# Where the second and third layer's input products are made in a four-layer trunk

## The chip, the cores and the metric

The kernel runs on one core of one Trainium2 chip. The time is device microseconds of one execution of the whole program; the median of the runs is given. The profile is one further execution, recorded by the hardware profiler. Five engines work beside each other and meet at semaphores: TensorE (PE) with its weight loads (PEld), VectorE (DVE), ScalarE (ACT), GpSimd (POOL) and SyncE (SP). SP issues most DMA transfers; POOL and ACT issue some.

## The reference

A trunk of four layers over 256 positions of width 1024, all in float32. Each layer adds three things to the residual h: a mixer (S5 state space in layers 0 and 3, attention with forget gates in layer 1, gated linear attention in layer 2), an MLP with squared ReLU, and a gated input embedding:

```python
for i in range(DEPTH):
    h = h + mixer_i(rmsnorm(h, norm_mix[i]))
    h = h + jnp.square(jax.nn.relu(rmsnorm(h, norm_mlp[i]) @ mlp_w1[i])) @ mlp_w2[i]
    gate = jax.nn.sigmoid(rmsnorm(h, norm_ple[i]) @ ple_gate[i])
    h = h + (p[i] @ ple_proj[i]) * gate
return rmsnorm(h, final_norm)
```

`p[i]` is an input of 256 positions by 256, `ple_proj[i]` a weight of 256 by 1024. Their product depends on nothing that the trunk computes, so it can be made at any time before the gate needs it.

## The kernel before

h stays in SBUF, transposed, as four tiles `HH` of 128 x 2 x 256. A big product streams its weight in units of 256 x 512 (512 KB). `unit` (L149) loads a unit into a tile `raw` (three buffers), ACT casts it to a rounded `whi` (L157), and DVE subtracts to get the rest, `wlo` (L159); each of the two has four buffers. The other operand is split the same way into two halves by `scaled` (L367, L368). `col` (L173 to L175) then makes three float32r matmuls in place of one exact product: hi x hi, hi x lo, lo x hi. `dense` runs such units over two column blocks and hands the finished PSUM tiles to an eviction function. The MLP uses a variant, `wide` (L209, L211).

An exact float32 matmul without the split is used in two places of the first S5 layer, "plain": the S5 input weights (`plain_block`, L261) and the input product of layer 0 (`plain_ple_proj`, L439 to L457). It needs no cast and no subtraction, and takes `raw` directly.

The embedding stage is `ple` (L459): it takes the input product `pp`, scales h, and makes the gate product with `ple_gate[l]`; the function `gate` (L472 to L479) multiplies by the normalisation, applies the sigmoid on ACT (L477), multiplies by `pp` (L478) and adds to h (L479). Where `pp` comes from differs by layer. For layers 0 and 3 it is made inside the S5 mixer (step p0 or p3) and waits in `pp_done`. For layers 1 and 2 `ple` calls `ple_proj` (L428) at its start: load `p`, split it on ACT and DVE, load and split two weight units, 48 matmuls, four copies out of PSUM (L436). So these products stand on PE between the last product of the MLP and the first product of the gate.

The first S5 layer is written out by hand as a list of steps, `FIRST` (L26). Four channel blocks b = 0 to 3 are passed through the steps w (input product, then the tile U by DMA), f (fetch of that block's S5 parameters, issued by POOL), i (input matrices and rotation, DVE), o (output matrices, DVE, with in-block products on PE, L922 to L927), s (states: 64 products, L972, then some ten DVE operations L708 to L989), y (outputs: products L1007, a GELU on ACT, transposes L1019, a split into `g`). Step p0 is the plain input product. After the list come the GLU products on `g` in `dense`, with the outputs of block 3 in their midst.

The order that the program gives is a priority: a scheduler with a simulated clock fixes each engine's order beforehand, taking among what it thinks ready the work that was written first. On the chip each engine follows that order strictly and waits where something isn't there. PSUM tiles are shared out by tags: `acc` and `wk` have three buffers, `po` and `mk` one each. The input products, the states of odd blocks and the transposes of `g` all take `acc`. `self.load` issues a transfer on SP behind the last weight unit.

Of the kernel before, what the change touches and what calls it, by code (L numbers as in the profile page):

```python
# [9 lines left out]
F32 = mybir.dt.float32  # L10
# [7 lines left out]
T, D, FF, DEPTH = 256, 1024, 4096, 4  # L18
# [4 lines left out]
        "acc": 3, "wk": 3, "po": 1, "mk": 1}  # L23


FIRST = "f0 w0 o0 w1 i0 w2 w3 f1 s0 i1 o1 s1 p0 f2 i2 y0 o2 s2 y1 f3 i3 o3 s3 y2"  # L26
LATER = "w0 i0 o0 w1 i1 o1 w2 s0 i2 w3 s1 p3 y0 o2 s2 i3 y1 o3 s3 y2"

HELD = 2
# [29 lines left out]
class Trunk:  # L59


    def __init__(self, ctx, tc, A):
        self.tc, self.nc, self.A = tc, tc.nc, A
        nc = self.nc
        pool = lambda name, **k: ctx.enter_context(tc.tile_pool(name=name, **k))
        self.const = pool("const", bufs=1)
        self.wp = pool("wp", bufs=4)
        self.sc = pool("sc", bufs=2)
        self.dram = pool("dram", bufs=1, space=bass.MemoryType.DRAM)
        self.sm = pool("sm", bufs=4)  # L70
        self.pp = pool("pp", bufs=4, space=PSUM)
        self.kept = self.ahead = self.last_unit = None
        self.lo_after = []
        self.pp_done = {}
        P = 128
        const = lambda name, shape, dt=F32: self.const.tile(shape, dt, name=name)
        self.lam = self.s5_load(0)
        self.gains = const("gains", [P, 3 * DEPTH + 1, 8])
        nc.sync.dma_start(self.gains, A["gains"])
        self.HH = [const(f"h{k}", [P, 2, T]) for k in range(4)]  # L80
        self.H = [self.HH[k // 2][:, k % 2] for k in range(8)]
        for k in range(4):
            nc.sync.dma_start(self.HH[k], A["xT"][k * 256:(k + 1) * 256, :].rearrange("(k p) t -> p k t", p=P))
        self.ident = const("ident", [P, P])
        make_identity(nc, self.ident)
        self.mhalf = const("mhalf", [P, 1])
        nc.gpsimd.memset(self.mhalf, -0.5)
        self.mean = const("mean", [P, 1])
        nc.gpsimd.memset(self.mean, 1.0 / D)
        self.ones = const("ones", [P, P])  # L90
        nc.gpsimd.memset(self.ones, 1.0)

        self.blk = const("blk", [P, 2])
        nc.gpsimd.affine_select(self.blk[:, 0:1], self.ones[:, :1], [[0, 1]], ALU.is_ge, 0.0, base=63, channel_multiplier=-1)
        nc.gpsimd.affine_select(self.blk[:, 1:2], self.ones[:, :1], [[0, 1]], ALU.is_ge, 0.0, base=-64, channel_multiplier=1)
        self.nblk = const("nblk", [P, 2])
        nc.gpsimd.tensor_scalar(self.nblk, self.blk, -1.0, None, ALU.mult)
        self.eye16 = const("eye16", [32, 16])
        nc.vector.tensor_tensor(self.eye16, self.ident[0:32, 0:16], self.ident[0:32, 16:32], ALU.add)
        self.zero = const("zero", [1, 512], BF16)  # L100
        nc.gpsimd.memset(self.zero, 0.0)
        self.halfpi = const("halfpi", [P, 1])
        nc.gpsimd.memset(self.halfpi, math.pi / 2)
        self.tms = [const(f"tm{i}", [P, 8, 4, 16]) for i in range(3)]
        for t in self.tms:
            nc.gpsimd.memset(t, 0.0)
# [329 lines left out]
        self.dense(x, A["ple_proj"][l], lambda n, ps: nc.scalar.copy(out[n // 2][:, n % 2], ps))  # L436
        return [out[n // 2][:, n % 2] for n in range(4)]

    def plain_ple_proj(self, l):  # L439

        nc, A = self.nc, self.A
        x = self.a2("praw", (128, 2, T))
        self.load(x, A["pT"][l].rearrange("(k p) t -> p k t", p=128))
        out = []
        for cb in range(2):
            raw = self.wp.tile([128, UK, 512], F32, name="raw", tag="raw", bufs=BUFS["raw"])
            self.last_unit = nc.sync.dma_start(raw, A["ple_proj"][l][:, cb * 512:(cb + 1) * 512].rearrange("(k p) n -> p k n", p=128))
            t = self.t4("pp", (128, 2, 2, T))
            for i in range(2):
                ps = self.psum((128, 2, T), "acc")  # L450
                for n in range(2):
                    for k in range(2):
                        c = (2 * i + n) * 128
                        nc.tensor.matmul(ps[:, n], raw[:, k, c:c + 128], x[:, k], start=k == 0, stop=k == 1)
                nc.scalar.copy(t[:, i], ps)
            out += [t[:, 0], t[:, 1]]
        return out  # L457

    def ple(self, l):  # L459
        nc, A = self.nc, self.A  # L460
        pp = self.pp_done.pop(l, None) or self.ple_proj(l)
        x = self.scaled(2 * DEPTH + l)
        sq = self.squares()
        v = {}

        def rows():
            v["rows"] = self.rstd_rows(sq)

        def rstd():
            v["r"] = self.rstd(v["rows"])  # L470

        def gate(n, ps):  # L472
            z = self.t2("z", (128, 2, T))

            for i in (slice(0, 1), slice(1, 2)) if l == DEPTH - 1 and n > 1 else (slice(0, 2),):
                nc.vector.tensor_tensor(z[:, i], ps[:, i], v["r"].unsqueeze(1).broadcast_to([128, i.stop - i.start, T]), ALU.mult)
                nc.scalar.activation(z[:, i], z[:, i], AF.Sigmoid)  # L477
                nc.vector.tensor_tensor(z[:, i], z[:, i], pp[n][:, i], ALU.mult)  # L478
                nc.vector.tensor_tensor(self.HH[n][:, i], self.HH[n][:, i], z[:, i], ALU.add)  # L479

        self.dense(x, A["ple_gate"][l], gate, mid={1: rows, 2: rstd}, tags=("acc", "wk"))
# [568 lines left out]
    def s5(self, l):  # L1050
        nc, A = self.nc, self.A
        j = l // 3
        first = self.kept is None
        us = []

        def w_in(b):
            w = A["s5_w_in"][j]
            ps = self.plain_block(x, w, b, q["mark"]) if first else self.block(x, w, b)
            u = self.t2("u", (128, 2, 4, 64))
            nc.vector.tensor_tensor(u.rearrange("x k s j -> x k j s"), ps.rearrange("x k (j s) -> x k j s", s=4),  # L1060
                                    r.rearrange("x (j s) -> x j s", s=4).unsqueeze(1).broadcast_to([128, 2, 64, 4]), ALU.mult)
            us.append(self.s5_inputs(u.rearrange("x k s j -> x k (s j)")))
# [14 lines left out]
        def make_in(b):  # L1077
            d0 = decay(b)
            if first:
                rot = drain(self.s5_rot(q, b))  # L1080
                return drain(self.s5_in(b, *parts[b][0:2])), rot, d0
            win = fetch(b, 0, (128, 2, 8, 64), "win")
            return [[win[:, i]] for i in range(2)], fetch(b, 1, (128, 2, 8, 64), "m4"), d0

        def make_out(b):
            if first:
                return self.s5_inside(b, *drain(self.s5_way_out(q, b, parts[b][2])))
            out = fetch(b, 2, (128, 2, 4, 8, 16), "m4")
            return [out[:, i] for i in range(2)], self.s5_lags(b, self.kept[0][b, 3, 0:32, 0:512].rearrange("x (p f) -> x p f", p=8), nc.sync)
# [16 lines left out]
        def step(what, b):  # L1106
            if what == "w":
                w_in(b)
            elif what == "f":
                parts[b] = self.s5_fetch(j, q, b)  # L1110
            elif what == "i":
                ins.append(make_in(b))
            elif what == "o":
                outs.append(make_out(b))
            elif what == "s":
                states.append(self.s5_states(b, us[b], *ins[b], first))
            elif what == "p":
                self.pp_done[l] = self.plain_ple_proj(l) if first else self.ple_proj(l)
            elif what == "y":
                gT.extend([] if gT else self.ktiles("g"))  # L1120
                self.s5_outputs(b, *states[b], *outs[b], gT)

        for t in (FIRST if first else LATER).split():
            step(t[0], int(t[1]))
# [122 lines left out]
```

## Time and profile before

| | |
|---|---|
| median of 3 runs | 1461.5 us (1461.08 to 1461.75) |
| the profiled execution, its own time | 1461.99 us |
| its span, first to last instruction | 1460.2 us |
| mean granted TensorE clock | 0.984 of full speed |
| DMA | 255.06 MB, 175 GB/s in the mean |

How to read the rows that follow. A line of the timeline has start and duration in us, the engine, the line of the program, the operation, the tile written and the tiles read, the shape, and a count; in brackets stands how long the engine was idle before it and what ended that. A row of the windows view has the window, its length, then for PE, PEld, DVE, ACT and POOL the busy us with the number of instructions in brackets, then the granted clock, the share of the 16 DMA engines and GB/s. A row of groups has the busy us, the mean ns of one, and the idle time before them with what ended it. PE's matmuls are pipelined: one can last 0.28 us by its record while the next starts 0.12 us after it, so start times tell the rate, durations don't.

### The profile page before, as it was taken

What the parts mean: (1) busy time and instruction counts of PE and PEld (TensorE: products, weight loads), DVE (VectorE), ACT (ScalarE), POOL (GpSimd) and SP (SyncE); (2) the same over time, 40 slices, a digit from 0 to 9 for tenths busy, and PEclk for the clock granted to TensorE, in tenths of its full rate; (3) what the DMA queues carried; (4) which work ended last, traced back from release to release, by engine and by line L of the source; (5) the groups of instructions that cost most, each with busy time, mean ns of one, the idle gap of its engine ahead of it and who ended that gap; (6) DMA issues with size and microseconds to landing.
All of it is one profiled execution on the core that took longest, in us unless ns stands there. A gap on an engine that the chain in (4) does not pass through costs nothing. (4 is left out here: it accounts for less than half of the span.)

```text
span 1460.2 us, 26622 instructions
## 1 busy us (share of the span) xinstructions
PE 1403.9 (96%) x10734; PEld 1266.9 (87%) x10734; DVE 1054.3 (72%) x1739; ACT 723.2 (50%) x1118; POOL 86.8 (6%) x142
## 2 busy tenths in 40 slices
PE   7889999999999999999999999999997899999998
PEld 6779988889999888888989588888997899888898
DVE  8994578767776578887676468886777946766665
ACT  3233565445655654545566455454563345545443
POOL 3100000010000000010004000100000000000020
PEclk9999999999999999999999999999999899999999
DMA  6623555566554347775555446774665446566551
GB/s 211 198 81 119 186 176 189 187 203 191 175 151 142 108 153 236 230 228 180 188 164 157 132 129 190 234 229 150 222 246 152 137 141 185 179 188 187 173 191 69
DMA packets 146347, 255.06 MB, mean 175 GB/s; under 512 B 24768, under 2 KB 35296, under 8 KB 146224
## 3 DMA queue, kind: packets, MB, share of 16 engines
q1 hardware_dynamic: 132912, 234.35, 50.8%
q0 software_dynamic: 5248, 17.31, 3.7%
q10 hardware_dynamic: 8064, 1.71, 0.6%
q8 instruction: 84, 1.38, 0.4%
q14 instruction: 39, 0.32, 0.1%
HBM read 242.68 MB, written 7.86 MB: 172 GB/s over the span
## 5 line engine op out<-in xcount | busy, mean ns | idle before, releaser
L159 DVE TENSOR_TENSOR wlo<-raw,whi 128x1024 fp32r<-128x1024 f32 x406 | 494.2, 1226 | 289.0 <-ACT whi L157 283.9
L157 ACT CAST whi<-raw 128x1024 fp32r<-128x1024 f32 x406 | 422.5, 1049 | 453.4 <-PE mk L209 77.7
L209 PE MATMUL wk<-x,whi 128*128 128x512 f32 x576 | 182.4, 401 | 7.5 <-DVE relu L220 7.5
L211 PEld LDWEIGHTS wk<-x,wlo 128*128 128x128 f32 x576 | 106.8, 190 | 23.1 <-issue 0.2
L209 PE MATMUL acc<-s,whi 128*128 128x512 f32 x384 | 118.5, 395 | 0.0
L211 PE MATMUL wk<-x,wlo 128*128 128x256 f32 x576 | 113.3, 281 | 0.0
L173 PE MATMUL acc<-x,whi 128*128 128x256 f32 x352 | 99.8, 288 | 4.6 <-DVE u L1060 2.9
L209 PEld LDWEIGHTS wk<-x,whi 128*128 128x128 f32 x576 | 92.2, 192 | 11.5 <-DVE relu L220 8.6
L174 PE MATMUL acc<-x,whi 128*128 128x256 f32 x352 | 100.3, 287 | 0.0
L175 PE MATMUL acc<-x,wlo 128*128 128x256 f32 x352 | 100.1, 286 | 0.0
L211 PEld LDWEIGHTS acc<-s,wlo 128*128 128x128 f32 x384 | 70.3, 188 | 15.8
L209 PE MATMUL mk<-x,whi 128*128 128x512 f32 x256 | 81.5, 395 | 0.0
L211 PE MATMUL acc<-s,wlo 128*128 128x256 f32 x384 | 74.3, 280 | 0.0
L173 PEld LDWEIGHTS acc<-x,whi 128*128 128x128 f32 x352 | 67.6, 194 | 6.4 <-issue 4.1
L175 PE MATMUL wk<-s,wlo 128*128 128x256 f32 x256 | 72.4, 283 | 0.0
L174 PE MATMUL wk<-s,whi 128*128 128x256 f32 x256 | 72.4, 283 | 0.0
L173 PE MATMUL wk<-s,whi 128*128 128x256 f32 x256 | 72.4, 283 | 0.0
L175 PEld LDWEIGHTS acc<-x,wlo 128*128 128x128 f32 x352 | 68.1, 194 | 0.1
L174 PEld LDWEIGHTS acc<-x,whi 128*128 128x128 f32 x352 | 68.0, 194 | 0.2
L209 PEld LDWEIGHTS acc<-s,whi 128*128 128x128 f32 x384 | 59.6, 189 | 1.4
L209 PE MATMUL po<-s,whi 128*128 128x512 f32 x192 | 60.7, 396 | 0.0
L209 PE MATMUL wk<-s,whi 128*128 128x512 f32 x192 | 60.1, 395 | 0.0
(399 smaller groups left out, 3376.0 us busy)
## 6 DMA issues: line engine op xcount, KB each, us to landing
raw<-mlp_w SPq DMA_DIRECT2D x256, 512.0 KB, 4.3
raw<-s_w_glu SPq DMA_DIRECT2D x32, 512.0 KB, 3.6
raw<-ple_gate SPq DMA_DIRECT2D x32, 512.0 KB, 3.6
raw<-fox_w_in SPq DMA_DIRECT2D x24, 512.0 KB, 3.8
raw<-gla_w_in SPq DMA_DIRECT2D x24, 512.0 KB, 3.6
raw<-s_w_out SPq DMA_DIRECT2D x16, 512.0 KB, 4.2
kept<-kept SPq DMA_DIRECT2D x12, 512.0 KB, 4.4
raw<-s_w_in SPq DMA_DIRECT2D x11, 512.0 KB, 4.7
```

Source lines behind the costliest of these rows:

```text
L157: nc.scalar.copy(hi, raw)
L159: self.last_lo = nc.vector.tensor_tensor(lo, raw, hi.bitcast(F32), ALU.subtract)
L173: mm(ps, hi, x[:, 0], start=first, stop=False, skip_group_check=True)
L174: mm(ps, hi, x[:, 1], start=False, stop=False, skip_group_check=True)
L175: self.last_mm = mm(ps, lo, x[:, 0], start=False, stop=last, skip_group_check=True)
L209: mm(ps[n], hi[:, i, s], v[i], start=first and i == 0, stop=False, skip_group_check=True)
L211: self.last_mm = mm(ps[n][:, 0], lo[:, i, s], v[i][:, 0], start=False, stop=last and i == UK - 1, skip_group_check=True)
```

## The change

The list `FIRST` gets two more steps: p1 between o2 and s2, and p2 between i3 and o3. Each makes the input product of layer 1 or 2 with the plain float32 code of p0, copies each of the four PSUM tiles on ACT into a small tile `pq`, and stores it to DRAM by a POOL DMA. In layers 1 and 2 `ple` no longer computes: `fetch_ple_proj` loads the four parts from DRAM into the two `pp` tiles. Layers 0 and 3 stay as they were. Layers 1 and 2 so use an exact float32 product in place of the three-matmul split.

```diff
-FIRST = "f0 w0 o0 w1 i0 w2 w3 f1 s0 i1 o1 s1 p0 f2 i2 y0 o2 s2 y1 f3 i3 o3 s3 y2"
+FIRST = "f0 w0 o0 w1 i0 w2 w3 f1 s0 i1 o1 s1 p0 f2 i2 y0 o2 p1 s2 y1 f3 i3 p2 o3 s3 y2"
...
-    def plain_ple_proj(self, l):
+    def plain_ple_proj(self, l, keep=False):
...
         out = []
+        store = None if keep else self.dram.tile([4, 128, 2, T], F32, name=f"pp{l}")
         for cb in range(2):
             raw = self.wp.tile([128, UK, 512], F32, name="raw", tag="raw", bufs=BUFS["raw"])
             self.last_unit = nc.sync.dma_start(raw, A["ple_proj"][l][:, cb * 512:(cb + 1) * 512].rearrange("(k p) n -> p k n", p=128))
-            t = self.t4("pp", (128, 2, 2, T))
+            if keep:
+                t = self.t4("pp", (128, 2, 2, T))
+                out += [t[:, 0], t[:, 1]]
             for i in range(2):
                 ps = self.psum((128, 2, T), "acc")
                 for n in range(2):
                     for k in range(2):
                         c = (2 * i + n) * 128
                         nc.tensor.matmul(ps[:, n], raw[:, k, c:c + 128], x[:, k], start=k == 0, stop=k == 1)
-                nc.scalar.copy(t[:, i], ps)
-            out += [t[:, 0], t[:, 1]]
+                n = 2 * cb + i
+                t = out[n] if keep else self.f2("pq")
+                nc.scalar.copy(t, ps)
+                if not keep:
+                    nc.gpsimd.dma_start(store[n], t)
+        if not keep:
+            self.pp_kept[l] = store
         return out
+
+    def fetch_ple_proj(self, l):
+        out = [self.t4("pp", (128, 2, 2, T)) for _ in range(2)]
+        for n in range(4):
+            self.load(out[n // 2][:, n % 2], self.pp_kept[l][n])
+        return [out[n // 2][:, n % 2] for n in range(4)]
...
-        pp = self.pp_done.pop(l, None) or self.ple_proj(l)
+        pp = self.pp_done.pop(l, None) or self.fetch_ple_proj(l)
...
-                self.pp_done[l] = self.plain_ple_proj(l) if first else self.ple_proj(l)
+                if first and b:
+                    self.plain_ple_proj(b)
+                else:
+                    self.pp_done[l] = self.plain_ple_proj(l, True) if first else self.ple_proj(l)
```

More of the change, by code (lines that the diff above doesn't have):

```diff
@@ L73, in __init__ @@
         self.lo_after = []
-        self.pp_done = {}
+        self.pp_done, self.pp_kept = {}, {}
         P = 128
```

## The prediction

> **What bounds the kernel now.** I read the page first: busy shares, then the forty slices.
>
> ```profile
> span 1460.2 us, 26622 instructions
> ...
> PE 1403.9 (96%) x10734; PEld 1266.9 (87%) x10734; DVE 1054.3 (72%) x1739; ACT 723.2 (50%) x1118; POOL 86.8 (6%) x142
> ...
> PE   7889999999999999999999999999997899999998
> ```
>
> TensorE (PE) works in nine tenths or more of nearly every slice; it lacks work in the first three (first S5 layer), around slice 31 (last S5 layer) and at the end. PE time taken out of a full slice comes off the end. PE time put into the first slices costs what doesn't fit into holes there.
>
> The windows view compares the four embedding stages, each from the last MLP product to the first product of what follows: layers 0, 1, 2, 3. The fifth row is layer 1's window for tile p alone; the sixth a group by line, 690 to 745 us.
>
> ```profile
> 373.80:399.00 25.20, 24.61 (x204) 24.39 (x204) 21.33 (x34) 16.80 (x25) 1.67 (x2) 1.00 0.54 170
> 712.30:743.50 31.20, 30.35 (x252) 30.09 (x252) 22.61 (x35) 20.19 (x31) 1.66 (x1) 1.00 0.54 172
> 1061.30:1092.50 31.20, 30.35 (x252) 30.09 (x252) 23.73 (x35) 20.23 (x30) 0.71 (x1) 1.00 0.71 254
> 1422.10:1446.80 24.70, 24.66 (x205) 24.43 (x204) 16.65 (x28) 12.42 (x22) 0.72 (x1) 1.00 0.20 65
> ...
> 712.30:743.50 31.20, 5.92 (x48) 5.77 (x48) 0.00 (x0) 0.00 (x0) 1.00 0.54 172
> ...
> L173 PE MATMUL acc<-x,whi 128*128 128x256 f32 x32 | 9.1, 288 | 0.8 <-ACT pp L436 0.8
> ```
>
> **Removed, layers 1 and 2.** Layers 0 and 3 have their input product done before the stage, so they are witnesses for it. 31.20 falls to 25.20 (layer 0) or 24.70 (layer 3): the 48 split products, 5.92, and the 0.8 in which the gate waits for ScalarE (ACT) to copy the last product out. I had feared that these products cover the MLP's tail (last eviction, h, scaled x) and that a wait appears in their place. Layer 0 has no such cover and PE is busy 24.61 of 25.20. I take 6.0 a layer, **12.0** in all; 6.5 by layer 3. With them go, each layer, two weight units' casts, the split of p and four copies: ACT and VectorE (DVE) have room there (about 20 of 31 us busy), so that counts nothing.
>
> **Fetched, layers 1 and 2.** Four 256 KB loads stand on SyncE's (SP) queue ahead of the gate's units, in place of 256 KB and two 512 KB loads. That is less data, the tiles' buffers are those of earlier MLP chunks, and the values are needed only at the gate's first eviction. Layer 2 moved 254 GB/s and its window was as long as layer 1's. Nothing; should a gate unit come late, that is the fourth rival.
>
> **Added, first S5 layer.** PE's timeline there:
>
> ```profile
> 60.99 1.99 PE L454 MATMUL acc<-praw,raw 128*128 128x256 f32 x8
> 66.92 3.52 PE L454 MATMUL acc<-praw,raw 128*128 128x256 f32 x8 [3.93 <-DVE R L708]
> ...
> 71.58 3.69 PE L454 MATMUL acc<-praw,raw 128*128 128x256 f32 x16 [0.65 <-DVE P L983]
> ...
> 82.82 0.30 PE L925 MATMUL mk<-qo,bx 128*32 128x64 f32 x2 [2.77 <-DVE qo L710]
> 83.42 2.08 PE L925 MATMUL mk<-qo,bx 128*32 128x64 f32 x20 [0.30 <-DVE qo L710]
> ...
> 92.50 2.03 PE L1007 MATMUL po<-qo,P 64*64 64x64 f32 x64
> 94.37 2.03 PE L1007 MATMUL po<-qo,W 64*64 64x64 f32 x64
> ...
> 96.65 1.42 PE L925 MATMUL mk<-qo,bx 128*32 128x64 f32 x22
> ...
> 104.30 1.15 PE L1007 MATMUL po<-qo,P 64*64 64x64 f32 x33
> 107.42 1.72 PE L1007 MATMUL po<-qo,P 64*64 64x64 f32 x30 [1.97 <-issue]
> ...
> 108.95 3.03 PE L1007 MATMUL po<-qo,W 64*64 64x64 f32 x63
> 111.91 0.39 PE L173 MATMUL wk<-g,whi 128*128 128x256 f32 x1
> ```
>
> A plain product leaves two records, so a layer's sixteen make 32. Sixteen records take 3.69 at most 0.23 apart; I take 0.22, since the last one's own end overlaps. Two layers: 64 x 0.22 = **14.1** on PE, more than the 12.0 removed. Everything turns on the holes. Stage windows (DVE busy is the third busy number, the clock follows POOL), then two fine ones:
>
> ```profile
> 60.00:70.00 10.00, 6.07 (x53) 4.88 (x48) 9.19 (x15) 4.32 (x9) 0.56 (x1) 0.83 0.42 114
> ...
> 80.00:90.00 10.00, 6.93 (x114) 5.93 (x115) 9.96 (x22) 3.11 (x8) 0.77 (x3) 0.83 0.01 2
> 90.00:100.00 10.00, 10.00 (x273) 9.16 (x271) 10.00 (x16) 3.35 (x6) 0.00 (x0) 1.00 0.21 47
> 100.00:110.00 10.00, 8.03 (x238) 7.95 (x236) 10.00 (x17) 1.31 (x2) 0.00 (x0) 0.88 0.56 176
> 110.00:120.00 10.00, 10.00 (x118) 9.73 (x116) 5.25 (x6) 3.18 (x4) 0.00 (x0) 0.95 0.22 73
> ...
> 80.00:83.00 3.00, 0.23 (x3) 0.14 (x2) 2.96 (x6) 0.67 (x2) 0.00 (x0) 1.00 0.00 0
> 83.00:86.00 3.00, 2.70 (x25) 2.42 (x24) 3.00 (x9) 0.00 (x0) 0.22 (x2) 0.62 0.00 0
> 86.00:105.00 19.00, 19.00 (x526) 17.53 (x526) 19.00 (x31) 7.10 (x13) 0.55 (x1) 0.97 0.33 97
> ```
>
> *p1* is emitted behind o2, whose in-block products are what PE waits for between 80.0 and 83.4, 2.77 + 0.30 = 3.1 us. PE keeps its emitted order among ready work, so p1 should fill this: **minus 3.1**. After the hole the clock is halved: 0.62 over 3 us and 0.97 over 19 us make about 3.4 us at half speed, and twenty products take 2.08 where twenty-two take 1.42 at full. A filled hole keeps the clock: **minus 1.6**. The rest of p1, 7.05 - 4.7 = 2.4, pushes s2's products back. DVE reaches those at 91.11 out of its own backlog:
>
> ```profile
> 91.11 1.27 DVE L708 TENSOR_TENSOR R<-wk,rot 128x512 f32<-128x512 f32 x2
> ```
>
> So about one of these microseconds shows on DVE, and PE is the later of the two.
>
> The Trainium skill, "TensorE: Matmul & The Clock Gate", "Part 1: The HAM clock gate", says that it takes an idle window of about 3.4 us to halve the clock; these rows agree with the length of the slow stretch, but 2.77 idle was enough. By that rule nothing but the hole itself would come back and the sum below would be -2.4 instead of -4.0.
>
> The 3.93 hole isn't filled: p0 itself waits there for a PSUM buffer of s1, and p1 takes the same three buffers.
>
> *p2* is emitted behind y1 and i3, ahead of o3 and s3. PE is busy 19.00 of 19.00 from 86 to 105, so all its 7.05 count. DVE's s3 starts some 9 us later; it works 5.25 of the ten from 110 and has room.
>
> *The stop at 105.* There PE waits for nothing but its instructions, 1.97, and then runs at half clock: 104.30 to 111.98 for what took 92.50 to 96.40, 3.8 us lost. Rows that bear on it: DVE frees three weight buffers in a row, three 512 KB loads fill the queues, and PE's instruction packets go through the same engines.
>
> ```profile
> 97.57 3.48 DVE L159 TENSOR_TENSOR wlo<-raw,whi 128x1024 fp32r<-128x1024 f32 x3
> ...
> 98.80:105.20 6.40, 6.40 (x204) 6.11 (x202) 6.40 (x10) 2.10 (x3) 0.00 (x0) 1.00 0.73 228
> ...
> q8 instruction: 84, 1.38, 0.4%
> ```
>
> With p1 and p2 in the buffer ring the GLU's loads come one by one, which speaks for the stop going; p2's stores, 1 MB, fall in the same time, which speaks against. Ends 0 and -3.8; nothing lies nearer to either, so I take the middle, **minus 1.9**. The Trainium skill, "Runtime: NRT & Kernel Launch", "Instruction fetch mechanics", calls a block's refill mostly hidden; here 1.97 was not. By the page the stop shouldn't come back and the sum would be -5.9.
>
> *DMA and other queues.* p1's 256 KB input may go out right behind p0's last weights, at 35 us, into a busy stretch in which DVE already waits for S5 coefficients:
>
> ```profile
> 40.00:50.00 10.00, 10.00 (x48) 8.81 (x47) 9.96 (x17) 1.22 (x4) 2.11 (x4) 1.00 0.78 219
> ...
> L861 DVE TENSOR_TENSOR wh<-bT,coef 128x1024 f32<-128x1024 f32 x4 | 4.9, 1220 | 3.1 <-DMA coef<-tab 3.1
> ...
> 34.72 0.40 SPq L447 DMA_DIRECT2D raw<-ple_proj  x1
> ...
> 63.43 0.56 POOL L852 DMA_DIRECT2D bc<-s_bc  x1 [6.33 <-ACT bx L914]
> ```
>
> At 219 GB/s it is 1.2 us; ends 0 and 1.2; **plus 0.5**, as not every transfer there is waited for. GpSimd's (POOL) eight stores each wait for a copy on ACT; behind them stands only work for layer 3, since this layer's last fetch, for block 3, goes out at 63.43. ACT gets eight copies and is under half busy.
>
> **Sum.** 14.1 - 3.1 - 1.6 - 1.9 + 0.5 - 12.0 = -4.0. The profiled execution took 1461.99, giving 1458.0; the median shown, 1461.5, is 0.5 lower: **1457.5**, with own range 1455.6 to 1459.4 from the stop's two ends.
>
> **Rivals.**
> 1. The stop stays whole and the coefficients cost 1.2: 14.1 - 4.7 + 1.2 - 12.0 = -1.4, 1460.1. For it: p2's stores.
> 2. DVE, not PE, sets the S5 stage (it is busy 10.00 of 10.00 from 90 to 110), and PE's order fills every hole: 3.93 + 0.65 + 3.1 + 1.97 = 9.6 and up to 1.7 of clock at each of three; that is 14.7, S5 grows by nothing: 1449.5. Against it: the 19.00 of 19.00.
> 3. Nothing is filled: PE's order, fixed beforehand, puts p1 where PE is busy and the hole stays; 14.1 + 1.1 - 12.0 = +3.2, 1464.7.
> 4. Slower by late weights. p1 and p2 use the three-buffer weight ring, so the GLU's second and third unit can be asked for only when p2's halves are done. If p2 ends right before the GLU's first products, PE waits for load, cast and subtraction, by these rows 3.6 + 1.0 + 1.2 = 5.8, and 1.7 of clock: 1457.5 + 7.5 = 1465.0. It decides once p2 ends less than 5.8 ahead of the GLU; I expect o3, s3 and y2 between, which took 96.65 to 111.98 before, 11.5 without the stop's 3.8.
>
> ```profile
> L159 DVE TENSOR_TENSOR wlo<-raw,whi 128x1024 fp32r<-128x1024 f32 x406 | 494.2, 1226 | 289.0 <-ACT whi L157 283.9
> L157 ACT CAST whi<-raw 128x1024 fp32r<-128x1024 f32 x406 | 422.5, 1049 | 453.4 <-PE mk L209 77.7
> ...
> raw<-s_w_glu SPq DMA_DIRECT2D x32, 512.0 KB, 3.6
> ```
>
> 5. The gate waits as long as the products took, for fetched values or weights, so nothing is gained: 1461.5 + 8.0 = 1469.5. Layers 0 and 3 speak against it.
>
> **Chances.** Forecast 0.46, rivals 0.15, 0.12, 0.10, 0.14, 0.03. A measurement of this kernel tells some 0.2% (2.9 us) from no change. Faster: four fifths of the forecast and rival 2, 0.49. Same: the rest of the forecast and rival 1, 0.24. Slower: 0.27. The range 1452 to 1465 holds the forecast, rivals 1 and 3, half of 4 and a third of 2, about 0.82.
>
> **What would show it.** Embedding stages of layers 1 and 2 at 25.2 with the gate right behind the MLP; 64 more plain records in the S5 layer, eight or more of them in the hole before o2's in-block products at full clock; the GLU's first product 8 us later than 111.9; the stop at 105 shorter or gone. A PE wait on wlo at the GLU's start, or a gate waiting for pp, would prove me wrong.

## The result and the profile after

The changed kernel takes 1468.2 us (median of 6 runs, 1466.4 to 1471.5) against 1460.3 for the kernel before on the same chip: a ratio of 1.0059, 95% interval 1.0042 to 1.0077. Run again beside the experiments it gave 1468.6 against 1457.4, 1.0073 (1.0060 to 1.0086). It is slower by six or seven tenths of a per cent; forecast was 0.3% faster, and the time lies above the range.

The profiled execution took 1466.69, against 1461.99 before: only 4.7 more where the medians are 8 to 11 apart. Before's profiled execution is one of its longer ones; two things in its trace that may have made it so are shown further down. First the page of after: span and busy shares, and PE's forty slices.

```profile
span 1464.9 us, 26581 instructions
...
PE 1405.9 (96%) x10702; PEld 1265.2 (86%) x10702; DVE 1048.8 (72%) x1733; ACT 718.0 (49%) x1112; POOL 90.0 (6%) x150
...
PE   7979999999999999999999999999997899999998
```

PE is busy 2.0 us longer than before (1405.9 for 1403.9) and idle 2.7 longer (1464.9 - 1405.9 for 1460.2 - 1403.9). The change exchanged PE time for PE time, nearly evenly, and made a few holes larger.

The windows view of after: layers 1 and 2, from the last MLP product to the first product behind the gate.

```profile
726.70:751.40 24.70, 24.60 (x205) 24.38 (x204) 19.72 (x33) 16.40 (x25) 0.71 (x1) 1.00 0.59 175
1069.50:1094.20 24.70, 24.66 (x205) 24.43 (x205) 21.50 (x34) 16.86 (x25) 0.71 (x1) 1.00 0.67 227
```

Both stages fell from 31.20 to 24.70, layer 3's length, with no wait for the fetched tiles: 13.0 us gained, 12.0 forecast. So the loss is elsewhere. The windows from the start to the GLU's first product, before and then after:

```profile
0.00:111.90 111.90, 93.36 (x1337) 81.64 (x1337) 101.60 (x257) 30.84 (x62) 19.19 (x50) 0.95 0.53 160
```

```profile
0.00:129.20 129.20, 107.38 (x1402) 92.78 (x1402) 99.32 (x253) 34.80 (x70) 23.43 (x58) 0.96 0.55 175
```

The first S5 layer grew by 17.3 where 8 was forecast. PE's busy time grew by 14.0, the 14.1 of the sum. Its idle time did not fall, as the holes to be filled would have made it; it grew from 18.5 to 21.8. PE's timeline of after shows which holes:

```profile
80.53 0.30 PE L939 MATMUL mk<-qo,bx 128*32 128x64 f32 x2 [2.76 <-DVE qo L724]
81.13 2.22 PE L939 MATMUL mk<-qo,bx 128*32 128x64 f32 x20 [0.30 <-DVE qo L724]
...
85.51 3.72 PE L457 MATMUL acc<-praw,raw 128*128 128x256 f32 x16
...
100.97 1.85 PE L1021 MATMUL po<-qo,W 64*64 64x64 f32 x56 [0.69 <-issue]
...
103.06 1.42 PE L939 MATMUL mk<-qo,bx 128*32 128x64 f32 x22
109.05 1.12 PE L1033 MATMUL acc<-ident,G 128*128 128x128 f32 x4 [4.57 <-ACT G L1030]
109.96 4.64 PE L457 MATMUL acc<-praw,raw 128*128 128x256 f32 x16
114.53 0.75 PE L939 MATMUL mk<-qo,bx 128*32 128x64 f32 x10
116.42 3.72 PE L457 MATMUL acc<-praw,raw 128*128 128x256 f32 x16 [1.15 <-DVE g L268]
...
129.18 0.39 PE L173 MATMUL wk<-g,whi 128*128 128x256 f32 x1
```

Three readings. (The counts in these rows are records; a float32 product leaves two.) The hole that p1 was to fill is still there, 2.76 + 0.30, and p1's first sixteen records come at 85.51, *behind* o2's. In place of the stop of 1.97 at 105 stands one of 0.69, at 100.97. And there is a new hole of 4.57 at 109.05, in which PE waits for ACT's copy G of block 1; p2's first sixteen records then take 4.64 where the next sixteen take 3.72, since part of them run at half clock (the granted clock is 0.73 in the mean from 109.0 to 114.6); at 116.42 comes another wait of 1.15.

Why G is late stands on ACT's timeline and on SP's issues:

```profile
98.26 1.05 ACT L157 CAST whi<-raw 128x1024 fp32r<-128x1024 f32 x1 [3.46 <-DMA raw<-s_w_glu]
107.45 1.04 ACT L157 CAST whi<-raw 128x1024 fp32r<-128x1024 f32 x1 [8.14 <-DMA raw<-s_w_glu]
108.41 0.59 ACT L1030 ACTIVATE G<-po 128x512 f32<-128x512 f32 x1
...
113.47 1.04 ACT L157 CAST whi<-raw 128x1024 fp32r<-128x1024 f32 x1 [3.66 <-DMA raw<-s_w_glu]
114.42 0.58 ACT L267 CAST g<-acc 128x512 fp32r<-128x512 f32 x1
```

```profile
73.03 16.60 SPq L448 DMA_DIRECT2D raw<-ple_proj  x2
...
103.81 0.37 SPq L153 DMA_DIRECT2D raw<-s_w_glu  x1
```

ACT works in a fixed order, and in it the cast of the GLU's second unit stands ahead of G. The unit was asked for at 103.81 only, since p2's two weight halves, asked for at 73.03 and some 16 us later, lay in two of the three ring buffers until p2 ran, from 109.96 on, and the third held the GLU's first unit until DVE had subtracted from it, at 103.78. ACT waited 8.14 us for it, and G, which PE had made ready at about 103, waited in the queue behind. The next unit does the same to the cast of g, which gives the 1.15.

### The profile page after: what moved, and what is told of

Same layout as the page of the kernel before. It is cut to its first block, busy times and chain, and to the rows that moved or that the text cites. A ratio compares the mean times of both kernels' runs of the same rounds, so it can differ in the third digit from the quotient of the medians.

```text
span 1464.9 us, 26581 instructions
## 1 busy us (share of the span) xinstructions
PE 1405.9 (96%) x10702; PEld 1265.2 (86%) x10702; DVE 1048.8 (72%) x1733; ACT 718.0 (49%) x1112; POOL 90.0 (6%) x150
## 4 chain that ended last, share of the span: by engine, by line
PE 83%; DVE 7%; DMA 4%; ACT 3%; issue 2%; SPq 0%; POOL 0%; DVEq 0%; ACTq 0%; POOLq 0%
PE wk L209 11%; PE acc L209 9%; PE acc L173 6%; PE acc L174 5%; PE wk L211 5%; PE acc L175 5%; PE acc L211 5%; PE wk L173 5%; PE wk L174 4%; PE wk L175 4%; PE mk L209 3%; PE po L209 3%; DVE wlo L159 2%; PE mk L211 2%; DMA raw<-mlp_w 2%
## 5 line engine op out<-in xcount | busy, mean ns | idle before, releaser
L157 ACT CAST whi<-raw 128x1024 fp32r<-128x1024 f32 x402 | 418.2, 1049 | 464.9 <-PE acc L174 77.4
```

The source lines that it names most:

```text
L157: nc.scalar.copy(hi, raw)
```

## The experiments

Each was timed in five rounds, with the kernel before on the same chip (medians 1457.4 to 1458.1). Where runs from different chips are set side by side, it is by their ratios to that. Beside the time stands the start of the GLU's first product (111.9 before, 129.2 after), which tells what the first S5 layer made of it, in the one execution that was profiled. The first three ran beside after once more:

> The changed kernel unaltered, on the same chip as the next three, so that they can be compared with it as well as with the kernel before. Expected: 1468 (1466.4 to 1471.5 so far), 0.6% above before.

It gave 1468.6, with that product at 129.9.

### Three first edits

```diff
-            raw = self.wp.tile([128, UK, 512], F32, name="raw", tag="raw", bufs=BUFS["raw"])
+            raw = self.wp.tile([128, UK, 512], F32, name="raw", tag="raw", bufs=BUFS["raw"]) if keep else self.t4("pw", (128, UK, 512), tag="x4")
```

> The two new steps' weights go to g and x tiles, which are free then, instead of the three-buffer weight ring; all else as after. Ring theory (the 4.57 us hole before y2's transposes comes from the GLU's second unit, which finds no free ring buffer, so that ACT's cast of it holds up the copy of G behind it): the cast no longer waits 8.1 us, the 4.57 hole and the 1.15 wait for an accumulator go, and 1 to 1.6 us of half clock with them: some 6.5 to 7 us less than after, about 1461.5. Rival (ACT holds G back for another reason, or PE is behind DVE there anyway): no change, 1468, and the hole stays at 4 to 5 us. Third: the GLU's loads go out three in a row again and the stop of 1.97 us with its half clock comes back: 6.5 - 3.8 = 2.7 less, 1465.5.

```diff
-FIRST = "... y0 o2 p1 s2 ..."
+FIRST = "... y0 p1 o2 s2 ..."
```

> Block 1's step is emitted ahead of o2 instead of behind it; its weights stay in the ring. Order theory (PE works off its emitted order strictly, so p1 behind o2 cannot fill the hole ahead of o2's products): sixteen or more plain records stand between 80 and 83.4, the hole of 2.76 + 0.30 goes and PE keeps its full clock there: 3.1 + 1.6 = 4.7 less than after, about 1463.5; the 4.57 hole further on stays, perhaps shorter. Rival (DVE sets o2 and s2, and PE has as much to wait for later): PE's hole only moves behind p1's products or to s2's, and the time stays at 1467 to 1468.

Both edits together:

> Both edits: block 1's step ahead of o2, and the two steps' weights in g and x tiles instead of the ring. If the two losses are separate, the gains add up: 4.7 + 6.5 = 11 less than after, about 1457, which is 3 to 4 less than before. If the second hole is only what the first left (DVE's backlog), the two together give no more than the larger one: 1461 to 1462.

Measured: 1464.9 (ratio 1.0048, 1.0033 to 1.0062), 1465.6 (1.0051, 1.0036 to 1.0065) and 1466.8 (1.0060, 1.0044 to 1.0075); GLU at 130.1, 129.3 and 131.0. None moved the GLU forward, so none bears out the mechanism that was expected; that they are 2 to 4 us below after goes with the last S5 layer, where PE's wait of 2.9 in after is 1.1 to 1.6 in these three (that wait is taken up below). Their timelines say why. Two rows of the run with other tiles, then two of the run with p1 written ahead of o2:

```profile
106.41 1.38 PE L1021 MATMUL po<-qo,P 64*64 64x64 f32 x40 [0.97 <-DVE P L999]
112.82 6.65 PE L457 MATMUL acc<-praw,pw 128*128 128x256 f32 x16 [5.03 <-DMA pw<-ple_proj]
```

```profile
81.59 1.30 PE L939 MATMUL mk<-qo,bx 128*32 128x64 f32 x20 [0.30 <-DVE qo L724]
...
109.31 1.11 PE L1033 MATMUL acc<-ident,G 128*128 128x128 f32 x4 [5.63 <-ACT G L1030]
```

With g and x tiles, the hole of 4.57 is gone, but the weights of p2 now come late themselves (5.03, and half clock behind it), and the scheduler has moved p2 into the midst of y2. With p1 written earlier, the scheduler put o2's in-block products ahead of it all the same: twenty of their records stand at 81.59, with p1 behind. The hole is only 1.08 + 0.30 in this profile, but the repetition of after, without the edit, has 1.15 + 0.30 there too. Where a step is *written* does not say where PE gets it.

### Gain alone and cost alone

The first leaves p1 and p2 out and fetches rows of x; the second makes them and lets the stages compute as before.

```diff
-            self.load(out[n // 2][:, n % 2], self.pp_kept[l][n])
+            self.load(out[n // 2][:, n % 2], self.A["xT"][n * 256:(n + 1) * 256, :].rearrange("(k p) t -> p k t", p=128))
```

> Gain alone: the steps p1 and p2 are left out, and the embedding stages of layers 1 and 2 fetch rows of the input x, of the same size, in place of the kept products (so the output lacks these two products). The first S5 layer is then as before. Expected if the stages are the whole gain: GLU's first product at 112, both stages at 24.7 instead of 31.2, 13.1 less than before. Rival: part of it is given back further on, because the stage no longer covers weights for the next layer: less than 10.

```diff
-        pp = self.pp_done.pop(l, None) or self.fetch_ple_proj(l)
+        pp = self.pp_done.pop(l, None) or self.ple_proj(l)
```

> Cost alone: p1 and p2 are made and stored in the first S5 layer as in after, and the stages of layers 1 and 2 compute their products again with the three-matmul split and use those. Expected: GLU's first product at 129, stages of 31.2, and 14 to 18 more than before (17.3 at the GLU, of which 14.3 were left at layer 1's stage). Rival: the rest of the run makes good for more of it, since weights run further ahead: under 10.

Measured: gain alone 1442.1, ratio 0.9895 (0.9878 to 0.9912), 12.8 to 17.8 us less; cost alone 1479.9, 1.0144 (1.0128 to 1.0161), 18.7 to 23.5 more. The gain is as large as expected or larger, and nothing is given back. One expectation failed: with the GLU's first product expected at 112, it came at 106.9, though PE's order up to there is that of before. So this profile is 5.0 us shorter in a stage that isn't altered: the stop is 1.36 there in place of 1.97, with no half clock behind it, and the hole ahead of o2's products is 1.19 + 0.30, at full clock, in place of 2.77 + 0.30. A GLU start from one profile can be off by that much. The cost is larger than expected: its GLU starts at 130.5, 18.6 later than in the profile of before and 23.6 later than in that of the gain alone, and no later layer makes up for any of that. Gain and cost together are +2 to +9, and after is +6 to +13.

### Is it the ring?

p2 written right behind p1, nothing else:

```diff
-FIRST = "... o2 p1 s2 y1 f3 i3 p2 o3 s3 y2"
+FIRST = "... o2 p1 p2 s2 y1 f3 i3 o3 s3 y2"
```

> p2 is written right behind p1 instead of behind i3; nothing else is changed. The ring is then free some 20 us earlier. Ring theory (GLU units that come late keep G in ACT's queue): no cast waits 8 us, the holes of 4.57 and 1.15 ahead of y2 go with their half clock, and GLU's first product comes 6 to 7 us sooner, at 122 to 123; the hole of 2.76 ahead of o2's products stays. Rival (DVE is behind there anyway, or the stop of 1.97 us and its half clock return because three GLU units go out in a row): 126 to 129.

And the cleaner trial, other tiles for the weights with PE's order in the first S5 layer that of after:

```diff
-            raw = self.wp.tile([128, UK, 512], F32, name="raw", tag="raw", bufs=BUFS["raw"])
+            raw = self.t4("pw", (128, UK, 512), tag="c4") if not keep else self.wp.tile([128, UK, 512], F32, name="raw", tag="raw", bufs=BUFS["raw"])
```

> The weights of p1 and p2 go to four other tiles (tag c4), not to the ring; TensorE's order in the first S5 layer stays word for word that of after, which the earlier trial with g and x tiles did not keep. Ring theory: the GLU's units are there early, ACT casts the second one without waiting, G of block 1 is copied in time, the holes of 4.57 and 1.15 and their half clock go and nothing else: GLU's first product at 122 to 123 in place of 129.2, 6 to 7 less than after; the holes of 2.21 and 2.76 stay. Rival (the holes are DVE's or the order's, and pairing p2 with p1 removed them by moving p2): GLU's first product at 127 or later with a hole of 3 us or more ahead of the transposes.

Measured: the pair 1457.1, ratio 0.9993 (0.9979 to 1.0008), GLU at 122.9; the other tiles 1462.1, 1.0031 (1.0015 to 1.0047), GLU at 122.0. Both GLU starts are where the ring theory had them. By the ratios the pair is 10 to 12 us below after, more than the 6 to 7 of GLU start, and the other tiles 4 to 6, a little less; the two differ by the last S5 layer, which comes below. PE and then ACT with the other tiles:

```profile
79.89 0.30 PE L939 MATMUL mk<-qo,bx 128*32 128x64 f32 x2 [2.76 <-DVE qo L724]
80.49 1.80 PE L939 MATMUL mk<-qo,bx 128*32 128x64 f32 x20 [0.30 <-DVE qo L724]
...
102.93 0.66 PE L1033 MATMUL acc<-ident,G 128*128 128x128 f32 x4
103.42 3.62 PE L457 MATMUL acc<-praw,pw 128*128 128x256 f32 x16
106.97 0.75 PE L939 MATMUL mk<-qo,bx 128*32 128x64 f32 x10
109.45 3.69 PE L457 MATMUL acc<-praw,pw 128*128 128x256 f32 x16 [1.73 <-DMA pw<-ple_proj]
```

```profile
96.60 1.05 ACT L157 CAST whi<-raw 128x1024 fp32r<-128x1024 f32 x1 [2.48 <-PE wk L986]
101.38 0.60 ACT L1030 ACTIVATE G<-po 128x512 f32<-128x512 f32 x1 [3.74 <-PE po L1021]
```

The same products in the same order on PE: G is copied 7.0 us sooner (101.38 for 108.41) since the cast ahead of it found its unit, and the transposes follow at 102.93 without a wait. ACT's order isn't quite that of after: three of the GLU's casts stand ahead of G in place of two. The pair shows the same with the weights left in the ring: three casts ahead of G, none of which waits more than 4.6, and G waits for PE. The hole of 2.76 stays, as it must by this theory.

### Is it the order? And a faster version

p1 and p2 right behind p0, with PSUM buffers that are free there:

```diff
-FIRST = "... s1 p0 f2 i2 y0 o2 p1 s2 y1 f3 i3 p2 o3 s3 y2"
+FIRST = "... s1 p0 p1 p2 f2 i2 y0 o2 s2 y1 f3 i3 o3 s3 y2"
...
-                ps = self.psum((128, 2, T), "acc")
+                ps = self.psum((128, 2, T), "wk")
```

> p1 and p2 are written right behind p0, and the plain products take PSUM buffers of the tag wk, which s0 has freed by then, instead of acc. Order theory (what the fixed order puts into a hole fills it): the holes of 1.40 + 2.21 at p0 go, those at o2's products shrink, the ring is free for the GLU early, so the 4.57 + 1.15 go too; PE's idle time up to the GLU falls from 21.2 to 10 or 11 and the half-clock stretches with it: GLU's first product at 116 to 118, 1449 to 1452 by this chip's before of 1457. Rival (DVE's own chain sets o2, s2 and o3, s3): PE's holes move behind the plain products and GLU's first product stays at 125 or later.

Before with that PSUM edit alone:

> Before, with one edit: p0's products take PSUM buffers of the tag wk in place of acc; p1 and p2 are left out and layers 1 and 2 make their products in their stages. It tells how much of the gain of the run with p1 and p2 behind p0 comes from that edit alone. If the holes at p0 merely move (DVE's chain sets o2 and s2): 0 to -2 against before, GLU's first product at 110 to 112. If they are a gain of their own: 4 to 6 less, GLU's first product at 106 to 108.

The version above with the weights in tiles of the tag c4, by the edit shown for the ring:

> p1 and p2 right behind p0 with buffers of the tag wk, as in the run before, and their weights in tiles of the tag c4, so that the GLU's units can come before them. If the stop of 1.93 us behind 115 came from the GLU's units falling on PE's instruction packets, it goes with its half clock: GLU's first product at 115 to 116, some 3 less than that run. If it comes from elsewhere, or the weights of p2 now come late: 118 to 121, the same or up to 3 more.

And with sixteen of p2's products fixed ahead of o2's:

```diff
-FIRST = "... s1 p0 f2 i2 y0 o2 p1 s2 y1 f3 i3 p2 o3 s3 y2"
+FIRST = "... s1 p0 p1 f2 i2 y0 p2 o2 s2 y1 f3 i3 o3 s3 y2"
...
-                ps = self.psum((128, 2, T), "acc")
+                ps = self.psum((128, 2, T), "acc" if keep else "wk")
```

> p1 behind p0 and p2 between y0 and o2, the two with PSUM buffers of the tag wk, p0 with acc; in TensorE's fixed order 16 products of p2 stand ahead of o2's in-block products. It does on the chip what the forecast took p1 to do: sixteen products in the hole before o2's products, so that hole (2.76 + 0.30) is gone or under 0.5, and the GLU's weights are in time. Expected GLU's first product at 117 to 120 and 1450 to 1453, some 6 less than before. Rival (DVE's chain sets o2, and the hole reappears behind p2's products or at s2): GLU's first product at 122 or later.

Measured: behind p0 1450.8, ratio 0.9948 (0.9930 to 0.9965), GLU at 118.7; the PSUM edit alone 1458.8, 0.9998 (0.9983 to 1.0013), GLU at 109.4; tiles of their own 1462.1, 1.0026 (1.0010 to 1.0043), GLU at 122.7; p2 ahead of o2 1450.0, 0.9945 (0.9926 to 0.9963), GLU at 117.8. The first and the last of these beat both kernels, the kernel before by 7 to 8 us. PE's timeline with the PSUM edit alone, and then with p2 ahead of o2:

```profile
82.48 0.42 PE L939 MATMUL mk<-qo,bx 128*32 128x64 f32 x2 [8.65 <-DVE qo L724]
```

```profile
85.67 4.58 PE L457 MATMUL wk<-praw,raw 128*128 128x256 f32 x20
90.09 0.60 PE L1033 MATMUL acc<-ident,G 128*128 128x128 f32 x4
90.53 2.76 PE L457 MATMUL wk<-praw,raw 128*128 128x256 f32 x12
93.21 0.39 PE L936 MATMUL mk<-zero 1*32 1x512 bf16 x1
93.53 1.97 PE L939 MATMUL mk<-qo,bx 128*32 128x64 f32 x32
...
116.62 1.20 PE L1021 MATMUL po<-qo,W 64*64 64x64 f32 x33 [1.12 <-issue]
```

Without p1 and p2, p0's earlier holes only gather into one of 8.65 ahead of o2's products: DVE's `qo` sets that moment, and the edit alone gains nothing. With the plain products in front, PE goes from 85.67 into o2's products without a wait and at full clock, and 14 us of products delay the GLU by only 117.75 - 109.44 = 8.3. That is the step that the forecast took p1 to do. What made the scheduler put p2 ahead of o2's products here, where it put p1 behind them when p1 was written in the same place, isn't shown: the two runs differ in the PSUM buffers (wk for acc) and in where p1 stands. The tiles of their own missed: p1's weights came late (a wait of 3.59 at 73.63), and a stop of 1.54 behind 119.8 was still there, so what makes PE's stops is not settled by it.

### One layer alone, and the last S5 layer

> Only layer 1's product is moved (p1 where after has it); layer 2 makes its own in its stage. By the sum that the traces of after gave: p1's 7.05 us all count, since the hole of 2.76 stays; its weights have left the ring by 93, so no GLU unit is late and the holes of 4.57 and 1.15 do not arise; the stop at 105 is shorter. GLU's first product at 116 to 118, one stage of 24.7: 0 to 3 less than before, 9 to 11 less than after. Rival (p1's stay in the ring is enough to delay the GLU): GLU's first product at 121 or later and no gain against before.

Measured: 1462.1, ratio 1.0021 (1.0004 to 1.0038), GLU at 118.0. The GLU is where it was expected; the time is 3 us more than before instead of 0 to 3 less. The difference lies in the last S5 layer. There one kernel after another falls into one of two groups, by these rows of PE's timeline (after, and then the pair):

```profile
1125.47 0.45 PE L986 MATMUL wk<-U,kept 64*64 64x64 f32 x8
1125.75 1.10 PE L1021 MATMUL po<-tm,U 64*64 64x64 f32 x32
1129.75 0.69 PE L986 MATMUL acc<-U,kept 64*64 64x64 f32 x8 [2.90 <-DMA tm<-kept]
```

```profile
1115.14 2.13 PE L986 MATMUL wk<-U,kept 64*64 64x64 f32 x64
...
1119.07 1.15 PE L1021 MATMUL po<-tm,U 64*64 64x64 f32 x32
1121.56 0.65 PE L986 MATMUL acc<-U,kept 64*64 64x64 f32 x15 [1.34 <-DVE u L1074]
```

After, its repetition and the runs with c4 tiles or one layer wait 2.9 to 3.1 here and then run at half clock; the others wait 1.6 or less, the run of the gain alone 2.3. Nothing of the change is in this layer: the scheduler came out with another order there. That its simulated clock goes on through the program would explain it, which no run shows. In after the state products of block 0 are broken up by products of w3. A last edit made them whole again, in after:

```diff
-LATER = "... o1 w2 s0 i2 w3 s1 p3 ..."
+LATER = "... o1 w2 w3 s0 i2 s1 p3 ..."
```

> After, with one edit in the list of the last S5 layer: w3 is written ahead of s0, so that block 0's 64 state products stand together in TensorE's order and are not broken up by w3's. The first S5 layer is as in after. If the 3 us that the last S5 layer lost come from that broken order (block 0's matrices stay in their single buffer some 2 us longer, so the next block's are fetched later and PE waits 2.9 us for tm behind them): the hole of 2.9 falls to 1.4 or less, and the stretch from the end of layer 2's MLP to the end of layer 3's first MLP wave, 197.6 to 198.3 so far, comes to 194 to 195; 2 to 3 less than after, 1465 to 1466. Rival (the hole is the fetch's own length, or the order is no cause): it stays at 2.5 or more and the stretch at 197 or more.

Measured: 1468.5, ratio 1.0074 (1.0054 to 1.0093). The stretch came to 194.8, as expected of the theory, but the hole is there still, at 3.19, and the time is no better, since the first S5 layer came out 3 us longer in that profile (GLU at 132.2). So the order matters, but not as I had put it: the stretch fell by 2.8 with the hole as long as before, so the hole is not where the 3 us went. PE and SP in that run:

```profile
1125.14 2.13 PE L986 MATMUL wk<-U,kept 64*64 64x64 f32 x64
1127.06 1.15 PE L1021 MATMUL po<-tm,U 64*64 64x64 f32 x32
1131.39 0.90 PE L986 MATMUL acc<-U,kept 64*64 64x64 f32 x12 [3.19 <-DMA tm<-kept]
```

```profile
1127.30 0.34 SPq L1081 DMA_DIRECT2D kept<-kept  x1
```

The next block's matrices are fetched when block 0's last state product has freed their single buffer, and PE is idle for what of the fetch nothing covers. In the pair fourteen products of w3 stand behind the state products and cover it, in before eighteen; in after and here none do. That fits the holes in all of these rows; it was not tried with a second buffer, and stays a reading. Where in this layer the 3 us go is open.

## Why the prediction was wrong

**Embedding stages, minus 12.0.** Right; 13.0, since layer 3's 24.7 was a better witness than layer 0's 25.2. The fetch costs nothing.

**64 records, plus 14.1.** Nearly right, and in part by luck. PE's busy time up to the GLU grew by 14.0, but that is a net: by their starts the 64 records, without half clock, took 15.1, 1.0 more (0.229 a record for the 0.22 of the sum, and 0.4 where PE went from these products to others and back), and half clock elsewhere, which is in the busy time, is less than in the profile of before.

**"PE keeps its emitted order among ready work, so p1 should fill this", minus 3.1, and minus 1.6 of clock.** This step failed, 4.7 of the error between these two profiles. From o2's first product to what follows o2's products it is 5.0 us in both. The premise holds only for what the scheduler takes to be ready in its simulated time; that this clock doesn't see the hole is how I read it. It fixed p1 behind o2's products, and the chip follows that. The run with p1 written earlier shows that writing alone does not decide it, the run with p2 ahead of o2 that such products, once fixed there, fill the hole. Rival 3 had the mechanism, with a chance of 0.10; the 1.1 in its sum has no row given for it. The worth of 4.7 was itself that of one profile: in the repetition of after the same hole is the 1.15 + 0.30 of these rows.

```profile
81.71 0.30 PE L939 MATMUL mk<-qo,bx 128*32 128x64 f32 x2 [1.15 <-DVE qo L724]
82.31 1.30 PE L939 MATMUL mk<-qo,bx 128*32 128x64 f32 x20 [0.30 <-DVE qo L724]
```

It is shorter there since PE comes to it later (80.17 for 77.39), and full clock follows.

**Weights at nothing in the sum.** The second failure, and the larger one: 4.57 and 1.15 of waits and 1.3 of half clock and gaps behind them, 7.0. The run with other tiles in after's order bears it out: its GLU starts 7.2 sooner, 0.7 of it won ahead of p1 and some 0.8 by the stop, and 1.73 of waiting for its own weights is still in it. The forecast did see the ring (rival 4, 0.14, priced at 7.5), but it looked for the wait at the GLU's first products and judged it by the 11.5 us between p2 and these. The wait came 20 us earlier and on another engine: ACT reached the cast of the second unit at 99 and stood, and with it G, which PE needed at 104. "PE waits on wlo at the GLU's start" never happened. That rival's size is near the measured one, at another place.

**The stop at 105, minus 1.9.** The sign was right and the size too small. Before, 104.30 to 111.91 took 7.6 and the same products take 4.1 in after; the stop of 0.69 costs 0.9 in an earlier block. That is minus 2.6.

**Coefficients, plus 0.5.** Not seen. o2's products began 2.3 us earlier than before (80.53 for 82.82), a gain that no term had, 2.8 from the forecast; PE's waits at p0 are shorter (1.40 and 2.21 for 3.93 and 0.65), and with them goes half clock behind the first (eight records in 1.96 for 3.52).

These make the first S5 layer's 17.3 out of the 8.0 forecast: 4.7 + 7.0 + 1.0 - 0.7 - 2.8 = 9.2 of the 9.3 between them. Each of the two profiles is one execution, and the 17.3 is more likely low than high: with 13.0 gained, the medians, 8 to 11 apart, ask for a cost of 21 to 24, the cost alone measured 18.7 to 23.5, and by the profile of the gain alone the GLU of the cost alone is 23.6 late.

**What was in no term.** The last S5 layer, 3.1 longer, by an order that the change touched only through the scheduler. Against it stand some 3 us that after gained between the GLU and the end of layer 1's MLP, among them the clock stretch shown below.

Rival 5's 1469.5 lies nearest to the 1468.2 measured, by luck: it has nothing gained in the embedding stages, and there the whole gain came.

## What to carry to other kernels

Work moved into a hole fills it only if the order that is fixed beforehand has it there: look at that order, not only at the place in the source. (Both faster versions also gave the moved work PSUM buffers that were free there; what that does by itself was not tried with p1 and p2.) When moved work borrows buffers of a ring, ask what the ring's next load holds up in *every* in-order queue on its way (here the cast on ACT, and behind it an unrelated copy that PE needed), not when its own products are due. And an edit under such a scheduler can shift a stage a thousand microseconds later; take the gain from the stages that it touches, but look through all of them.

## What was not expected of the hardware

Short holes halve the clock at times and at times they don't, and their length doesn't decide it. The same twenty microseconds of layer 0's MLP, before and then in the run of the gain alone, each with one hole ahead of its second wave (1.77 and 1.82 us):

```profile
308.10:328.10 20.00, 18.23 (x95) 15.51 (x94) 10.90 (x14) 8.79 (x13) 3.78 (x7) 0.91 0.70 206
```

```profile
321.28 0.73 PE L209 MATMUL wk<-x,whi 128*128 128x512 f32 x2 [1.77 <-DVE relu L220]
```

```profile
303.40:323.40 20.00, 18.18 (x104) 15.54 (x103) 10.90 (x14) 9.31 (x14) 3.78 (x7) 1.00 0.68 198
...
316.57 0.74 PE L209 MATMUL wk<-x,whi 128*128 128x512 f32 x2 [1.82 <-DVE relu L220]
```

0.91 over 20 us is about 1.8 us lost, behind the shorter of the two holes; in after, with 1.42 at this place, the clock is 1.00 as well. This may be one reason why before's profiled execution is longer than its median. By the Trainium skill, "TensorE: Matmul & The Clock Gate", "Part 1: The HAM clock gate", the gate watches an activity window of about 3.4 us; a hole of 1.77 was enough here. The price, where it is paid, is steadier than single rows make it look. Behind the hole of 2.76 ahead of o2's products, twenty records took 2.22 in after and 1.80 in the run with other tiles, but from o2's first product to p1's first it was 4.98 and 4.93. In the repetition of after, with 1.15 and full clock, it was 3.43: half clock cost some 1.5 us there. An estimate that counts half clock behind a short hole should carry both ends, nothing and such a price.
